# The first unit of the first product as eight plain products instead of seven combined ones

## The chip, the cores and the metric

The kernel runs on one core of a Trainium2 chip. The metric is the device time of one execution in microseconds (us); lower is better. "TensorE" or PE is the matrix engine, "VectorE" or DVE and "ScalarE" or ACT are the two engines that do sums, copies and the activation, POOL and SP mainly issue transfers (DMA).

## The reference

```python
# x: 16 x 512 x 768, w1: 768 x 3072, b1: 3072, w2: 3072 x 768, float32
y = np.matmul(x, w1) + b1
y = 0.5 * y * (1.0 + erf(y / np.sqrt(2.0)))        # GELU
return np.matmul(y, w2)
```

## The kernel before

The 8192 rows of x are worked on in blocks of 1024. In a block, the first product is cut into 12 units, one for each 256 columns of w1. A unit is a 2 x 2 block product: A11, A12, A21, A22 are quarters of the x block (512 rows by 384), B11 to B22 are quarters of the unit's weight (384 by 128). It is done with seven block products in place of eight, at the price of sums (a form of Strassen's scheme). On TensorE one block product is three matmuls of 128x512.

```python
# sums of x (DVE), made once for a block:     S1, S2, A21 (overwritten), S4
ops = ((S1, A21, A22, ADD), (S2, S1, A11, SUB), (A21, A11, A21, SUB), (S4, A12, S2, SUB))

# sums of the weight (DVE), made for each unit; T1 overwrites B12 in place
for d, a, b in ((T3, B22, T1), (T1, T1, B11), (T2, B22, T1), (T4, B21, T2)): ...   # d = a - b

# the seven products of a unit: p -> (operand from x, operand from the weight)
{1: (A11, B11), 2: (A12, B21), 3: (S4, B22), 4: (A22, T4),
 5: (S1, T1),   6: (S2, T2),   7: (A21, T3)}
```

The products go to six PSUM banks (bX and bY twice, bW, bZ); engine copies between banks (`copy_xy`: bX to bY; after P6: bY to bZ) let later products add to an earlier sum. Each unit overlaps with the one before it:

```python
def period(i, j, fill):              # i: this unit, j: the one before
    if i and i.g:
        p1(i); copy_xy(i)            # unit 0's P1 and P2 are done by the start code
    if j: p7(j)
    fill(1)                          # fill: DVE sums for later units, loads
    if i: p5(i)
    fill(2)
    if j: p3(j)
    fill(3)
    if i: p6(i)
    if j: j.right_done()             # GELU
    fill(4)
    if j: p4(j)
    fill(5)
    if i and i.g: p2(i)
    fill(6)
```

The start loads eight tiles of x (128 rows each) and the first weights, transposes the tiles on TensorE and copies them out of PSUM. Meanwhile "spins", matmuls on zeros that compute nothing, are there to keep TensorE busy, so that it keeps its clock.

```python
spin(9)
for t in range(4):
    ...                                       # cast tile t
    transpose_pe(0, t)
    spin(2 if t < 3 else 6)
nc.vector.tensor_copy(...)                    # weight 0, first half of its rows: cast by DVE
nc.scalar.copy(...)                           # second half: cast by ACT
prep_wt(0); flush(soon)                       # four subtractions on weight 0
first = Unit1(0, 0, 0)
p1(first, 0, KQ)
copy_xy(first)
for t in range(4, 8):
    transpose_pe(0, t, nc.vector.tensor_copy if t == 5 else nc.scalar.copy)
    if t % 2:
        x_sums(0, soon, top if t == 5 else bottom, (0, 1)); flush(soon)
    if t < 7:
        spin(2)
p2(first)
spin(3)
...                                           # other x sums; then period(first, None, ...)
```

## Time and profile before

| | before |
|---|---|
| median of the first three runs | 857.49 us (856.77 to 858.31) |
| span of the profiled run | 856.2 us |
| TensorE busy | 850.1 us, 99% |
| VectorE / ScalarE busy | 76% / 49% |

The profile's page first. Its busy row gives busy us, share of the span and number of instructions for each engine; the other row gives shares of the chain of waits, the chain of work that ended last.

```profile
PE 850.1 (99%) x6307; PEld 560.7 (65%) x6307; DVE 653.8 (76%) x1108; ACT 421.2 (49%) x682; POOL 80.6 (9%) x131
PE 97%; DMA 2%; ACT 0%; DVE 0%; SPq 0%; issue 0%
```

TensorE bounds the kernel. The table by stages says where it is not full: the columns are the stretch, its length, PE's busy time and matmuls, granted TensorE clock (1.00 is full), DMA share, GB/s.

```profile
0.00:20.00 20.00, 18.06 (x103) 1.00 1.08 227
20.00:40.00 20.00, 19.96 (x97) 1.00 1.29 193
```

Only the first 20 us have room, and a good part of what is busy there is spins. So the start is read one row at a time: start us, busy us, engine, source line, operation, output and input, count, and in brackets the engine's idle time before and what ended it. L663 is a spin, L294 a transpose, L369 a product of a unit.

```profile
13.96 0.51 PE L294 MATMUL bT<-ident,arena 128*128 128x128 f16 x6
14.31 0.81 PE L369 MATMUL bX<-arena 128*128 128x512 f16 x3
14.95 0.38 PE L663 MATMUL bY<-arena 128*128 128x512 f16 x1
15.17 0.38 PE L663 MATMUL bZ<-arena 128*128 128x512 f16 x1
15.38 0.38 PE L663 MATMUL bY<-arena 128*128 128x512 f16 x1
15.95 0.81 PE L369 MATMUL bW<-arena 128*128 128x512 f16 x3 [0.19 <-DVE arena L179]
16.59 0.81 PE L369 MATMUL bY<-arena 128*128 128x512 f16 x3
17.24 0.81 PE L369 MATMUL bX<-arena 128*128 128x512 f16 x3
18.06 0.81 PE L369 MATMUL bY<-arena 128*128 128x512 f16 x3
18.71 0.81 PE L369 MATMUL bW<-arena 128*128 128x512 f16 x3
...
23.44 0.81 PE L369 MATMUL bW<-arena 128*128 128x512 f16 x3
...
28.05 0.81 PE L369 MATMUL bW<-arena 128*128 128x512 f16 x3
```

The last tile is transposed at 13.96, P2 of unit 0 follows at 14.31, then three spins and a wait: P5 of unit 0 (bW, 15.95) needs the sum S1, which needs the copy of tile 7. Five products of unit 0 (P5, P6, P7, P3, P4) are still to do there. Because matmuls overlap, three of them advance the start of the next group by 0.65 us, not by the 0.81 shown. Each bW row is P5 of a unit: unit 0 at 15.95, unit 1 at 18.71, unit 2 at 23.44, unit 3 at 28.05. From there the distance is 4.53 us per unit: TensorE is full. So **P5 of unit 3** marks how much the start cost.

ScalarE's copy of tile 7 (L296) ends at 14.51 + 0.80 = 15.31:

```profile
10.30 0.83 ACT L676 CAST arena<-arena 128x768 f16<-128x768 f32 x1
...
14.51 0.80 ACT L296 COPY arena<-bT 128x768 f16<-128x768 f16 x1 [0.18 <-PE bT L294]
```

### The profile page before, as it was taken

Reading aid. Unit: us, or ns where it says so; the run is one execution under the profiler, and the core shown is the slowest. Engines: PE = TensorE matmul, PEld = TensorE weight load, DVE = VectorE, ACT = ScalarE, POOL = GpSimd, SP = SyncE. Lnnn points to the kernel's source line nnn. Section 1 sums busy time; section 2 is a strip of 40 time slices with the busy share of each in tenths; the row PEclk is TensorE's granted clock in tenths of the full one; section 3 lists DMA queues with packets and bytes.
Section 4 is the critical chain, followed back from the end, with each engine's and each line's share of the span. In section 5 each row is a group of like instructions: output and inputs, shape, how many; then the busy total and the mean of one; then the engine's idle time right before and its main releaser. Section 6 shows DMA issues by size and latency. Waiting matters only on the chain.

```text
span 856.2 us, 16201 instructions
## 1 busy us (share of the span) xinstructions
PE 850.1 (99%) x6307; PEld 560.7 (65%) x6307; DVE 653.8 (76%) x1108; ACT 421.2 (49%) x682; POOL 80.6 (9%) x131
## 2 busy tenths in 40 slices
PE   9999999999999999999999999999999999999998
PEld 4444445666544798448974499645995459944698
DVE  5765676756447998579986799677996689956998
ACT  5777762111177512875138732477215771267611
POOL 5021100000100001100020000200002100010000
PEclk9999999999999999999999999999999999999999
DMA  9996895659889798996979879897998959967398
GB/s 225 223 236 96 242 192 188 235 167 284 186 242 319 192 324 324 266 291 209 335 279 307 246 257 333 277 286 222 301 345 257 337 153 324 356 218 272 97 304 288
DMA packets 143265, 219.03 MB, mean 256 GB/s; under 512 B 61692, under 2 KB 84148, under 8 KB 143188
## 3 DMA queue, kind: packets, MB, share of 16 engines
q1 hardware_dynamic: 117968, 180.62, 65.6%
q0 software_dynamic: 25184, 37.36, 20.9%
q8 instruction: 49, 0.80, 0.4%
q14 instruction: 28, 0.23, 0.1%
q10 hardware_dynamic: 36, 0.01, 0.0%
HBM read 180.30 MB, written 47.87 MB: 266 GB/s over the span
## 4 chain that ended last, share of the span: by engine, by line
PE 97%; DMA 2%; ACT 0%; DVE 0%; SPq 0%; issue 0%
PE bY L369 21%; PE bY L461 15%; PE bX L369 14%; PE bX L461 10%; PE bW L369 7%; PE bZ L369 7%; PE bY L409 5%; PE bZ L461 5%; PE bW L461 5%; PE bX L409 4%; PE bZ L409 2%; PE bW L409 2%; DMA arena<-w1s 1%; DMA arena<-in_x_dram 1%; PE bT L294 0%; ACT arena L296 0%
## 5 line engine op out<-in xcount | busy, mean ns | idle before, releaser
L179 DVE TENSOR_TENSOR arena<-arena 128x768 f16<-128x768 f16 (+4 forms) x620 | 392.7, 664 | 10.6 <-PE bW L409 2.8
L369 PEld LDWEIGHTS <-arena 128*128 128x128 f16 x2016 | 196.5, 98 | 230.5 <-issue 1.3
L461 PEld LDWEIGHTS <-arena 128*128 128x128 f16 x3528 | 292.1, 98 | 8.3
L369 PE MATMUL bY<-arena 128*128 128x512 f16 x864 | 218.9, 379 | 0.1
L539 DVE TENSOR_TENSOR arena<-bY,arena 128x512 f32<-128x512 f32 (+1 forms) x104 | 70.8, 681 | 144.7 <-PE bY L369 88.7
L369 PE MATMUL bX<-arena 128*128 128x512 f16 x576 | 141.5, 379 | 0.6 <-DMA arena<-w1s 0.6
L532 ACT COPY bY<-bX 128x512 f32<-128x512 f32 (+1 forms) x146 | 80.3, 550 | 125.0 <-DVE arena L510 87.7
L385 ACT ACTIVATE arena<-arena,b1t 128x1024 f16<-128x1024 f32 x96 | 110.4, 1151 | 57.2 <-DVE arena L567 57.2
L461 PE MATMUL bY<-arena 128*128 128x192 f16 x1500 | 138.3, 246 | 0.0
L552 ACT COPY arena<-bW 128x512 f32<-128x512 f32 (+1 forms) x146 | 80.8, 553 | 95.1 <-PE bW L461 43.3
L409 PEld LDWEIGHTS <-arena 128*128 128x128 f16 x672 | 65.8, 98 | 44.2
L461 PE MATMUL bX<-arena 128*128 128x192 f16 x1020 | 93.1, 246 | 0.0
L567 DVE TENSOR_TENSOR arena<-bZ,arena 128x512 f32<-128x512 f32 (+1 forms) x104 | 70.7, 680 | 25.5 <-PE bZ L369 18.4
L369 PE MATMUL bW<-arena 128*128 128x512 f16 x288 | 77.8, 379 | 0.2 <-DVE arena L179 0.2
L369 PE MATMUL bZ<-arena 128*128 128x512 f16 x288 | 77.8, 379 | 0.0
L390 ACT ACTIVATE arena<-bX,b1t 128x512 f16<-128x512 f32 x96 | 65.4, 681 | 7.5 <-PE bX L369 7.5
L493 POOL DMA_DIRECT2D out_dram<-arena x42 | 30.6, 729 | 394.8 <-DVE arena L563 288.3
L390 ACT ACTIVATE arena<-bY,b1t 128x512 f16<-128x512 f32 x96 | 64.7, 674 | 0.0
L284 POOL DMA_DIRECT2D arena<-in_x_dram x60 | 32.4, 544 | 273.2 <-DMA arena<-arena 194.0
L585 DVE COPY bZ<-bY 128x512 f32<-128x512 f32 (+1 forms) x67 | 45.8, 683 | 6.1
L409 PE MATMUL bY<-arena 128*128 128x384 f16 x288 | 49.6, 326 | 0.0
L461 PE MATMUL bZ<-arena 128*128 128x192 f16 x504 | 48.5, 246 | 0.0
(43 smaller groups left out, 331.2 us busy)
## 6 DMA issues: line engine op xcount, KB each, us to landing
arena<-w2s SPq DMA_DIRECT2D x294, 288.0 KB, 4.6
arena<-w1s SPq DMA_DIRECT2D x72, 672.0 KB, 5.8
out_dram<-arena POOLq DMA_DIRECT2D x42, 384.0 KB, 4.8
w2s<-arena SPq DMA_DIRECT2D x49, 288.0 KB, 4.4
arena<-in_x_dram POOLq DMA_DIRECT2D x60, 192.0 KB, 6.7
w1s<-arena SPq DMA_DIRECT2D x12, 672.0 KB, 8.2
out_dram<-arena SPq DMA_DIRECT2D x21, 384.0 KB, 3.2
arena<-in_w_dram POOLq DMA_DIRECT2D x17, 384.0 KB, 8.1
```

The costliest lines, as they stand in the source:

```text
L179: nc.vector.tensor_tensor(out=o, in0=a, in1=b, op=op)
L284: nc.gpsimd.dma_start(out=xhs[t], in_=xr[:, sb * 8 + t, :])
L369: nc.tensor.matmul(out=dst[:, 0:RH], lhsT=w1_op(self.wt, slot)[:, c, :], rhs=a[:, c, :], start=first and c == 0, stop=c == self.C - 1, ski ...
L385: nc.scalar.activation(out=self.G[1][:, hi, :, :], in_=self.tmp, func=GELU, bias=b1t[:, 2 * hi + 1:2 * hi + 2])
L390: nc.scalar.activation(out=self.G[0][:, hi, row, :], in_=bank[:, 0:RH], func=GELU, bias=b1t[:, 2 * hi:2 * hi + 1])
L409: nc.tensor.matmul(out=dst[:, 0:N2], lhsT=a, rhs=w[:, :, c, :], start=first and c == 0, stop=c == self.C - 1, skip_group_check=True)
L461: nc.tensor.matmul(out=dst[:, t * N4:(t + 1) * N4], lhsT=a, rhs=w[:, c, :], start=first and c == 0 and t == ts[0], stop=c == NQ - 1, skip_ ...
L532: nc.scalar.copy(out=bY[u.g % 2][:, 0:u.F], in_=bX[u.g % 2][:, 0:u.F])
L539: nc.vector.tensor_tensor(out=u.c22(), in0=bY[u.g % 2][:, 0:u.F], in1=w[:, 0:u.F], op=ADD)
L552: nc.scalar.copy(out=w[:, 0:u.F], in_=bW[:, 0:u.F])
L567: nc.vector.tensor_tensor(out=u.c12(), in0=bZ[:, 0:u.F], in1=w[:, 0:u.F], op=ADD)
L585: nc.vector.tensor_copy(out=bZ[:, 0:u.F], in_=bY[u.g % 2][:, 0:u.F])
```

## The change

The intent: unit 0 of the first block is computed plainly, C = A1 B1 + A2 B2 with eight block products. That is one product more, but none waits for a sum, so some can be done while tiles 4 to 7 still arrive. Weight 0's subtractions leave the start; they are done at unit 3, because unit 0 of the second block needs them.

```diff
-            spin(2 if t < 3 else 6)
+            spin(2)
 ...
-        prep_wt(0)
-        flush(soon)
-        first = Unit1(0, 0, 0)
-        p1(first, 0, KQ)
-        copy_xy(first)
-        warm = warm[1:]
-        for t in range(4, 8): ...            # transposes, sums, spin(2)
-        p2(first)
-        spin(3)
+        def plain(dst, row, side, half):
+            slot = ((B11, T1), (B21, B22))[half][side]      # the T1 slot still holds B12
+            for c in range(KQ):
+                nc.tensor.matmul(out=dst[:, 0:RH], lhsT=w1_op(wts[0], slot)[:, c, :],
+                                 rhs=blocks(0)[2 * row + half][:, c, :],
+                                 start=half == 0 and c == 0, stop=half == 1 and c == KQ - 1, ...)
+        plain(bX[0], 0, 0, 0)
+        transpose_pe(0, 4)
+        plain(bX[0], 0, 0, 1)
+        transpose_pe(0, 5, nc.vector.tensor_copy)
+        x_sums(0, soon, top, (0, 1)); flush(soon)
+        transpose_pe(0, 6)
+        plain(bY[0], 0, 1, 0)
+        transpose_pe(0, 7)
+        x_sums(0, soon, bottom, (0, 1)); flush(soon)
+        plain(bY[0], 0, 1, 1)
+        spin(2)
+        for row, banks in enumerate(((bX[0], bY[0]), (bW, bZ))):
+            for side in range(2):
+                if row:
+                    plain(banks[side], row, side, 0)
+                    plain(banks[side], row, side, 1)
+                plain_done(banks[side], row, side)          # GELU straight from PSUM
+        prep_wt(1)
+        ...                                   # other x sums
 ...
             if slot == 4:
+                if pos == 3:
+                    prep_wt(0)
 ...                                          # cuts: unit 0 leaves the loop over units
```

The spins now write bX[1] and bY[1]. That is not cosmetic: P6 and P7 add to a value that ScalarE has copied into bY. The Trainium skill ("PSUM — Partial Sum Buffer", "The four PSUM rules") says that VectorE and ScalarE writes neither set nor clear the bits which decide whether a matmul adds or overwrites; a matmul adds to such a value where the bit is set, as it is after any matmul wrote there. A spin does that for bY[1], and the plain products do it for bY[0] and bZ.

More of the change, by code (lines that the diff above doesn't have):

```diff
@@ L577, in p6 @@
             u.mm(6, bY[u.g % 2], False, 0, u.C)
-            on_act = u.g == 0 or isinstance(u, Unit3) or (isinstance(u, Unit1) and u.sb >= ONE and u.g % 2)
+            on_act = isinstance(u, Unit3) or (isinstance(u, Unit1) and u.sb >= ONE and u.g % 2)
             if isinstance(u, Unit3) and u.add is not None:
@@ L610, in period @@
                 return
-            if i and i.g:
+            if i:
                 p1(i, 0, i.C)
@@ L630, in period @@
             fill(5)
-            if i and i.g:
+            if i:
                 p2(i)
@@ L657 @@
             load_wt(n)
-        warm = [bY[0], bY[1], bZ]
         def spin(n):
             for k in range(n):
-                nc.tensor.matmul(out=warm[k % len(warm)][:], lhsT=zero[:, 0, 0:P], rhs=zero[:, 0, :],
+                nc.tensor.matmul(out=(bX[1], bY[1])[k % 2][:], lhsT=zero[:, 0, 0:P], rhs=zero[:, 0, :],
                                  start=True, stop=True, skip_group_check=True)
@@ L673 @@
                 nc.scalar.copy(out=b1t[:], in_=bW[:, 0:2 * NH])
-            spin(2 if t < 3 else 6)
+            spin(2)
         nc.vector.tensor_copy(out=w1_raw(wts[0])[:, 0:KQ, :], in_=wf[:, 0:KQ, :])
         nc.scalar.copy(out=w1_raw(wts[0])[:, KQ:2 * KQ, :], in_=wf[:, KQ:2 * KQ, :])
-        prep_wt(0)
-        flush(soon)
-        first = Unit1(0, 0, 0)
-        p1(first, 0, KQ)
-        copy_xy(first)
-        warm = warm[1:]
-        top, bottom = slice(0, 2 * P), slice(2 * P, RH)
-        for t in range(4, 8):
-            transpose_pe(0, t, nc.vector.tensor_copy if t == 5 else nc.scalar.copy)
-            if t % 2:
-                x_sums(0, soon, top if t == 5 else bottom, (0, 1))
-                flush(soon)
-            if t < 7:
-                spin(2)
@@ L691 @@
-        p2(first)
-        spin(3)
-        for r in (top, bottom):
-            x_sums(0, soon, r, (2,))
-        flush(soon)
-        for r in (top, bottom):
-            x_sums(0, soon, r, (3,))
+        def plain(dst, row, side, half):
[3 more added lines that the diff above has]
+                                 rhs=blocks(0)[2 * row + half][:, c, :],
+                                 start=half == 0 and c == 0, stop=half == 1 and c == KQ - 1,
+                                 skip_group_check=True)
@@ new lines, in plain_done @@
+        def plain_done(dst, row, side):
+            nc.scalar.activation(out=Gs[0][side][:, 0, row, :], in_=dst[:, 0:RH], func=GELU,
+                                 bias=b1t[:, side:side + 1])
+        top, bottom = slice(0, 2 * P), slice(2 * P, RH)
+        plain(bX[0], 0, 0, 0)
+        transpose_pe(0, 4)
+        plain(bX[0], 0, 0, 1)
+        transpose_pe(0, 5, nc.vector.tensor_copy)
+        x_sums(0, soon, top, (0, 1))
+        flush(soon)
+        transpose_pe(0, 6)
+        plain(bY[0], 0, 1, 0)
@@ new lines @@
+        transpose_pe(0, 7)
+        x_sums(0, soon, bottom, (0, 1))
+        flush(soon)
+        plain(bY[0], 0, 1, 1)
[7 more added lines that the diff above has]
+        prep_wt(1)
+        last = [soon.pop()]
+        for k in (2, 3):
+            for r in (top, bottom):
+                x_sums(0, soon, r, (k,))
@@ L700 @@
+        flush(soon)
+        soon += last
         seq = ([(0, k) for k in range(7)] +
@@ L732, in fill_a @@
             if slot == (1 if pos < at[1, 0] else 4) and pos + 1 < len(seq) and seq[pos + 1][0] == 0:
-                s4 = [soon.pop(0), soon.pop(0)] if pos == 0 else []
                 prep_wt(seq[pos + 1][1])
-                soon[2:2] = s4
             if slot == 4:
+                if pos == 3:
+                    prep_wt(0)
                 for m, c in ((21, 9), (22, 0), (23, 3), (23, 6)):
@@ L755, in fill_a @@
                     sums((0, 1100, 0, 0, 1500)[slot])
-            elif slot in (1, 2, 4, 5) and (pos, slot) != (0, 2):
+            elif slot in (1, 2, 4, 5):
                 sums((0, 600, 300, 0, 600, 300)[slot])
@@ L905 @@
         for g, (kind, sb, k) in enumerate(units):
-            cur = kind(g, sb, k) if g else first
+            if g == 0:
+                loads_a(0)
+                continue
+            cur = kind(g, sb, k)
             if g < len(seq):
```

## The prediction

> **What bounds the kernel.** TensorE: 850.1 of 856.2 us busy (99%, busy table), 97% of the chain of waits, granted clock 1.00. By the stage table PE is full from 20 us to the tail, except 0.6 us at a weight reload. Only the first 20 us (PE 18.06 busy, partly warm-up "spins" that compute nothing) can give time back; afterwards PE runs at a fixed period (timeline: 4.53 us per seven-product unit).
>
> **Removed, added, moved** (timeline of the first 30 us; a product, three 128x512 matmuls, takes 0.65 us; six transposes 0.33; a spin 0.21).
> Unit 0 goes from 7 to 8 products (+0.65 us of PE), but they need no sums. Before, PE filled the waits for x tiles 4 to 7 (transposes at 11.35, 12.11, 12.98, 13.96; the last two waited for loads), for the copy of tile 7 (ends 15.31) and for the first sum with 9 spins; when that sum was done (15.95), five products of unit 0 were left. After, three more products fit between the transposes, so at the copy of tile 7 (about 15.3, fixed by the same loads) four are left, ending near 18.0.
>
> Then unit 1: P1 at 18.0, P5, P6 (waits about 0.2 us for the ScalarE copy, queued behind four GELUs), P2, then P1 of unit 2, P7 of unit 1, and P5 of unit 2 at about 22.2. Before it started at 23.44, and P5 of unit 3 at 28.05; I expect the latter at 26.7 to 27.1, 1.0 to 1.35 us earlier.
>
> DVE loses four subtractions of weight 0 there (1.54 us); they come back at units 3 to 4. DVE then has 3.6 + 1.5 us of work in a 4.53 us period, lagging about 0.5 us, against slack of about 0.45 us at the copy to bZ and 1 us at the c22 sum: cost to PE 0 to 0.2 us. DVE is the risk earlier too: six x sums (0.52 each), weight-1 subtractions (0.36 each) and the first bZ copy (0.7), which P7 of unit 1 waits for, end near 21.4, just when PE gets there (21.45). Weights 1, 2, 3 seem to land at 16.2, 18.2, 20.2 (POOL's waits), early enough.
>
> **Critical path.** All the PE gain is on it; nothing later absorbs it, as later loads are issued from program positions. The Trainium skill ("TensorE: Matmul & The Clock Gate", Part 1) says that PE needs about 3.4 us of sustained activity for full rate and loses it after an idle window as long. The trace agrees with the first: spins are 0.43 us apart until about 5 us, then 0.21. Idle gaps after stay under 0.7 us, so I expect no loss.
>
> **Predicted:** 856.3 us (gain 1.2, 0.14%), range 855.2 to 857.4, which includes the run-to-run spread (856.8 to 858.3 before). Faster by over 2%: 0.003; within 2%: 0.992; slower by over 2%: 0.005.
>
> **Shown right by:** first product near 10.5; row-1 products from about 15.4 to 18.0 without gap; P5 of unit 3 around 27; two PE matmuls fewer in all (3 more, 5 spins fewer); period still 4.53 at units 4 and 5. **Shown wrong by:** a PE wait above 0.4 us on DVE at unit 1's bZ copy, a stall at the deferred weight-0 subtractions, waits on weight loads, or matmuls at 0.43 us (clock lost).
>
> **What would make it wrong.** DVE or ScalarE queue order costing more than 0.2 us at units 1 to 4, eating the gain to about 0; or the clock falling with fewer spins (+1 to 3 us).

## The result, and the profile after

Four sets of executions were made, each with before and after on the same chip. All are fast: none is over 1.5% above the fastest of its kernel. All outputs are right. The ratio is the mean time of one kernel's fast runs over that of the other's fast runs of the same rounds, so not quite the ratio of the medians.

| set | before: median (runs) | after: median (runs) | ratio, 95% interval |
|---|---|---|---|
| 1, the result | 857.58 (4) | 856.54 (4) | 0.9989, 0.9970 to 1.0008 |
| 2, run after_again | 858.72 (11) | 856.22 (6) | 0.9985, 0.9969 to 1.0002 |
| 3, run after_third | 858.49 (11) | 857.67 (6) | 0.9998, 0.9979 to 1.0018 |
| 4, run after_fourth | 857.73 (9) | 856.07 (5) | 0.9978, 0.9965 to 0.9992 |

The mean of all 21 runs after is 856.98, of all 35 before 858.11: 1.1 us less (0.13%), with a standard error of 0.4 us worked out from the spread of both groups; without the one run of 862.01 us it is 1.4 us.

The same two rows of the page, and of the table by stages, after:

```profile
PE 848.3 (99%) x6299; PEld 560.3 (66%) x6299; DVE 652.0 (76%) x1106; ACT 419.6 (49%) x680; POOL 81.1 (9%) x131
PE 98%; DMA 1%; POOL 0%; issue 0%; DVE 0%
```

```profile
0.00:20.00 20.00, 17.89 (x101) 1.00 1.08 227
20.00:40.00 20.00, 20.00 (x103) 1.00 1.28 197
```

Note the trap: TensorE is *less* busy in the first 20 us than before. Busy time does not show the gain, as a spin counts as busy. The rows of the timeline do (L680 is a plain product, L662 a spin):

```profile
14.07 0.51 PE L294 MATMUL bT<-ident,arena 128*128 128x128 f16 x6
14.42 0.81 PE L680 MATMUL bY<-arena 128*128 128x512 f16 x3
15.07 0.38 PE L662 MATMUL bX<-arena 128*128 128x512 f16 x1
15.28 0.38 PE L662 MATMUL bY<-arena 128*128 128x512 f16 x1
15.50 1.46 PE L680 MATMUL bW<-arena 128*128 128x512 f16 x6
16.80 1.46 PE L680 MATMUL bZ<-arena 128*128 128x512 f16 x6
18.09 0.81 PE L369 MATMUL bX<-arena 128*128 128x512 f16 x3
18.74 0.81 PE L369 MATMUL bW<-arena 128*128 128x512 f16 x3
19.56 0.81 PE L369 MATMUL bY<-arena 128*128 128x512 f16 x3
...
21.50 0.81 PE L369 MATMUL bY<-arena 128*128 128x512 f16 x3
22.15 0.81 PE L369 MATMUL bW<-arena 128*128 128x512 f16 x3
...
26.68 0.81 PE L369 MATMUL bW<-arena 128*128 128x512 f16 x3
```

Four products of unit 0 are left at 15.50 and end at 18.09 without a gap. P5 of units 1, 2, 3 starts at 18.74, 22.15, 26.68. ScalarE's copy of tile 7 ends at 14.62 + 0.80 = 15.42:

```profile
14.62 0.80 ACT L296 COPY arena<-bT 128x768 f16<-128x768 f16 x1 [0.20 <-PE bT L294]
```

So the *stretch* from the end of that copy to P5 of unit 3 fell from 28.05 - 15.31 = 12.74 us to 26.68 - 15.42 = 11.26 us, by 1.48. Three parts make it up:

- Before, TensorE took up unit 0's remainder 0.64 us after the copy (15.95), waiting for a sum; after, 0.08 us (15.50). 0.56 us.
- From there to P5 of unit 3 there are 18 products before and 17 after. One product is 0.65 us (4.53 / 7).
- 18 products are 11.65 us of the 12.10 between 15.95 and 28.05, so 0.45 us were gaps; 17 are 11.0 of the 11.18 after, so 0.18 (P6 of unit 1 waits 0.17, at 19.56). 0.27 us.

The first and the third part are read from these rows; no run changed one of them alone.

VectorE after, first behind the copy of tile 7 and then at unit 3, where the deferred subtractions are:

```profile
15.45 5.09 DVE L179 TENSOR_TENSOR arena<-arena 128x768 f16<-128x768 f16 x12 [0.65 <-ACT arena L296]
...
20.47 0.70 DVE L585 COPY bZ<-bY 128x512 f32<-128x512 f32 x1
...
30.00 1.79 DVE L179 TENSOR_TENSOR arena<-arena 128x384 f16<-128x384 f16 x5
31.71 0.68 DVE L539 TENSOR_TENSOR arena<-bY,arena 128x512 f32<-128x512 f32 x1
```

VectorE has no gap from 15.45 until 21.8. The copy to bZ, for which P7 of unit 1 waits, ends at 21.17, and P7 starts at 21.50: 0.33 us of slack. At 30.00 five subtractions stand where there was one, and no idle time is left before the c22 sum (31.71), which adds the banks that P7 and P5 of a unit left; before, it was 1.13 us:

```profile
32.85 0.69 DVE L539 TENSOR_TENSOR arena<-bY,arena 128x512 f32<-128x512 f32 x1 [1.13 <-PE bY L369]
```

The two first profiles differ by 2.1 us, more than the start explains (1.37 by the clock). The rest is a wait of the profile before, for a weight that is fetched again (w1s), that the first profile after happens not to have. The product before it starts at 384.07, so this one is 1.39 - 0.65 = 0.74 us late; the idle time in brackets, 0.57, is less, as it counts from the modelled end of a matmul:

```profile
385.46 0.82 PE L369 MATMUL bX<-arena 128*128 128x512 f16 x3 [0.57 <-DMA arena<-w1s]
```

### The profile page after: what moved, and what is told of

It reads as the page before. It is cut to its first block, busy times and chain, and to the rows that moved or that the text cites. A ratio compares the mean times of both kernels' runs of the same rounds, so it can differ in the third digit from the quotient of the medians.

```text
span 854.1 us, 16173 instructions
## 1 busy us (share of the span) xinstructions
PE 848.3 (99%) x6299; PEld 560.3 (66%) x6299; DVE 652.0 (76%) x1106; ACT 419.6 (49%) x680; POOL 81.1 (9%) x131
## 4 chain that ended last, share of the span: by engine, by line
PE 98%; DMA 1%; POOL 0%; issue 0%; DVE 0%
PE bY L369 22%; PE bY L461 15%; PE bX L369 14%; PE bX L461 10%; PE bZ L369 7%; PE bW L369 7%; PE bY L409 5%; PE bZ L461 5%; PE bW L461 5%; PE bX L409 4%; PE bZ L409 2%; PE bW L409 2%; DMA arena<-in_x_dram 1%; POOL arena L284 0%; PE bT L294 0%; PE bY L680 0%
## 5 line engine op out<-in xcount | busy, mean ns | idle before, releaser
L369 PE MATMUL bY<-arena 128*128 128x512 f16 x855 | 216.7, 379 | 0.0
L369 PE MATMUL bX<-arena 128*128 128x512 f16 x570 | 139.7, 379 | 0.0
```

The lines of the kernel that those rows point to most:

```text
L369: nc.tensor.matmul(out=dst[:, 0:RH], lhsT=w1_op(self.wt, slot)[:, c, :], rhs=a[:, c, :], start=first and c == 0, stop=c == self.C - 1, ski ...
```

## The experiments

The whole time scatters by more than the effect, so the verdicts rest on one profile each and on the stretch defined above, which leaves out when tile 7 came. The table has every profile. "Rest" is span minus P5 of unit 3; "reload" is the recorded idle time of TensorE on w1s, which is smaller than the delay it stands for (0.57 for 0.74 above).

| run | copy of tile 7 ends | stretch | rest | reload | span |
|---|---|---|---|---|---|
| before | 15.31 | 12.74 | 828.15 | 0.57 | 856.2 |
| before_again | 16.97 | 12.74 | 827.49 | 0 | 857.2 |
| before_third | 15.19 | 12.74 | 828.27 | 0.57 | 856.2 |
| after | 15.42 | 11.26 | 827.42 | 0 | 854.1 |
| after_again | 15.20 | 11.26 | 827.94 | 0.50 | 854.4 |
| after_third | 15.97 | 11.26 | 828.87 | 1.19 | 856.1 |
| after_fourth | 15.26 | 11.26 | 827.58 | 0 | 854.1 |
| fewer_spins | 15.45 | 12.73 | 829.22 | 1.12 | 857.4 |
| two_moved | 16.94 | 12.56 | 827.70 | 0.29 | 857.2 |
| sums0_early | 15.05 | 12.40 | 829.05 | 1.32 | 856.5 |
| row1_halves | 15.53 | 10.88 | 831.69 | 2.85 | 858.1 |
| halves_act | 15.16 | 10.21 | 828.93 | 0.39 | 854.3 |
| halves_act_2 | 14.95 | 10.21 | 829.54 | 0.84 | 854.7 |
| halves_wq | 15.56 | 10.21 | 828.73 | 1.23 | 854.5 |

The theory: the copy of tile 7 fixes when the rest can run, and the change leaves fewer products, and no sum, behind it. Rivals: the gain comes from spins taken out of TensorE's way; from the plain form wherever it stands; from the deferral of weight 0's subtractions alone; or the difference of the totals is only scatter.

### The two kernels again

> The kernel before once more, for the spread of the start in the profile. P5 of unit 3 (the bW product near 28 us) started at 28.05 us in the first profile; every theory expects 28.05 within 0.15. The wait of 0.74 us on a weight reload near 385 us need not come back, as it is taken to be chance; if it comes back at the same place, it belongs to the kernel.

> The changed kernel once more, with more executions. P5 of unit 3 started at 26.68 us in its first profile: 26.7 within 0.15 expected. If the gain is the 1.37 us of the start and nothing else, the ratio of times is 0.9984 (856.2 for 857.6). If the whole 2.1 us of the two first profiles belonged to the change, 0.9975.

Both stretches came back to 0.01 us. But before_again was 1.66 us late at P5 of unit 3 (29.71, where I expected 28.05 within 0.15: a miss), with the whole delay ahead of the copy of tile 7. ScalarE in before_again:

```profile
12.73 0.83 ACT L676 CAST arena<-arena 128x768 f16<-128x768 f32 x1 [2.37 <-DMA arena<-in_w_dram]
13.46 0.58 ACT L532 COPY bY<-bX 128x512 f32<-128x512 f32 x1
13.98 0.79 ACT L296 COPY arena<-bT 128x768 f16<-128x768 f16 x1
```

The second half of weight 0 came at 12.7 us, where the first profile had it by 10.3. The copy of tile 4 (13.98), whose transposes had begun at 11.49, had to wait behind that cast. The Trainium skill ("TensorE: Matmul & The Clock Gate", Part 1, on queue depths) says that the queues of ACT and DVE are strictly first in, first out; these rows agree. The reload wait near 385 us was absent here, so it is not a fixed part of the kernel before. The ratio of after_again, 0.9985, is the one that the start alone gives (0.9984).

### Fewer spins

```diff
 # in the kernel before
-            spin(2 if t < 3 else 6)
+            spin(2)
-            if t < 7:
-                spin(2)
-        spin(3)
+        spin(2)
```

> The kernel before with 19 spins in place of 30 (as many as after), still seven combined products. Theory (the copy of x tile 7 and then the first sum set the start, spins only fill waits): P5 of unit 0 stays at 15.95 and P5 of unit 3 at 28.05, within 0.15. Rival (the gain comes from the spins taken out of TensorE's way): P5 of unit 3 comes up to 1.3 us earlier, near 26.7. If the clock falls for lack of work, matmuls at 0.43 us show it.

The stretch was 12.73 us, as in the kernel before; P5 of unit 0 started at 16.09, the copy of tile 7 ended 0.14 us later than in the first profile, and P5 of unit 3 at 28.18. No product ran at the slow rate. The spins only fill waits; taking eleven out gains nothing.

### Two products moved back behind tile 7

```diff
 # in the kernel after
-        plain(bY[0], 0, 1, 0)
+        spin(3)
         transpose_pe(0, 7)
 ...
-        plain(bY[0], 0, 1, 1)
+        spin(3)
         spin(2)
 ...
-                if row:
+                if row or side:
```

> The kernel after with the two products of the second side of row 0 (bY) moved from between the transposes to behind the copy of tile 7; three spins stand in each one's old place. The same eight products, so the same work. Theory (what counts is how many products are left when tile 7 is there): six in place of four are left, P5 of unit 3 comes 2 x 0.648 = 1.30 us later, at 27.98 (0.1 to 0.2 less if the moved products close an existing wait). Rival (the plain form itself, without sums and copies, brings the gain, wherever it stands): stays at 26.7 within 0.3.

By the clock P5 of unit 3 started at 29.50, but this execution again had the late weight half (the copy of tile 7 ended at 16.94). Counted from there the stretch was 12.56 us, 1.30 more than the 11.26 of the kernel after: two products at 0.65, to the hundredth. That the late weight itself does not change the stretch is known from before_again. So eight plain products bring nearly nothing (0.18 us) if two more of them stand behind tile 7; what counts is how many are left there. This run also has the deferred subtractions, so the deferral alone is not the gain either. The copy of tile 7 and P5 of unit 3:

```profile
16.14 0.80 ACT L296 COPY arena<-bT 128x768 f16<-128x768 f16 x1 [0.18 <-DVE arena L179]
...
29.50 0.81 PE L369 MATMUL bW<-arena 128*128 128x512 f16 x3
```

### Weight 0's subtractions back at the start

```diff
 # in the kernel after: behind the x sums of the start, no longer at pos 3
+        prep_wt(0)
         flush(soon)
         soon += last
```

> The kernel after with the four subtractions of weight 0 put back into the start (before the last subtraction of weight 1) in place of unit 3. If the deferral matters: VectorE runs without a gap from 15.45 to 20.5 us in the kernel after, and 4 x 0.36 = 1.44 us more push the copy to bZ of unit 1 from 20.47 to 21.9 and P7 of unit 1 from 21.50 to 22.65, a TensorE wait of about 1.1 us; P5 of unit 3 at 27.8 or a little later. Rival (VectorE has room there, deferral only tidies): P5 of unit 3 stays at 26.7 within 0.2.

VectorE's row of sums was four longer, and TensorE waited. The rows are VectorE's, then TensorE's:

```profile
15.09 6.53 DVE L179 TENSOR_TENSOR arena<-arena 128x768 f16<-128x768 f16 x16 [0.68 <-ACT arena L296]
21.53 0.69 DVE L585 COPY bZ<-bY 128x512 f32<-128x512 f32 x1
```

```profile
22.28 0.81 PE L369 MATMUL bY<-arena 128*128 128x512 f16 x3 [0.98 <-DVE bZ L585]
```

P7 of unit 1 waited 0.98 us, and the stretch rose by 1.14 to 12.40 us, which leaves 0.34 of the gain of 1.48. P5 of unit 3 by the clock was 27.45, below the 27.8 that I gave, as tile 7 was copied 0.37 us earlier here. Against this place the deferral is a needed part of the change, though it shows no gain of its own: VectorE had 0.33 us of room there, and 1.4 us of work would have gone into it. Note that the run does not put them where they stood before (11.17 us, ahead of tile 5): T1 overwrites B12, which the plain products still read until 17.4 us. VectorE stood idle for 3.02 us there in the kernel after (until 12.99), so with a buffer of its own for T1 they might fit; no run tried that.

### Going further: the second row in halves

```diff
 # in the kernel after; plain_cols does 256 of the 512 columns, tiles 4 and 5 (top) or 6 and 7
         plain(bX[0], 0, 0, 0)
+        plain(bY[0], 0, 1, 0)
         transpose_pe(0, 4)
 ...
         transpose_pe(0, 7)
 ...
-        spin(2)
+        plain_cols(bW, 0, top)
+        plain_cols(bZ, 1, top)
 ...                                # behind the copy of tile 7 only plain_cols(..., bottom)
```

> A try to go further: the kernel after with its second-row products cut into two halves of 256 columns, the half for tiles 4 and 5 done before the copy of tile 7 in place of the last two spins, and one product of row 0 moved ahead of tile 4. TensorE alone would finish unit 0 at 17.0 in place of 18.09. If VectorE's unbroken row of sums (to 20.5 us) and the copy to bZ behind it are the next limit, P7 of unit 1 still waits until about 21.1 to 21.2, and P5 of unit 3 gains only 0.3 to 0.5 (26.2 to 26.4). If TensorE's own row is the limit, it gains 1.0 (25.7).

> As row1_halves, and the copy to bZ of unit 1 is done by ScalarE, so it need not queue behind VectorE's sums. If VectorE's queue was the limit of row1_halves, P5 of unit 3 comes at 25.6 to 25.8, 0.9 to 1.1 us ahead of the kernel after; time against the kernel before 0.9972 (2.4 us). If not, it equals row1_halves.

> halves_act again, beside halves_wq and the kernel after on one chip. The stretch from the copy of tile 7 to P5 of unit 3 was 10.21 us, 1.05 below the kernel after: 10.2 within 0.05 again, and a median 1.0 us below the kernel after (or up to 0.5 away from that by the spread of the weight reloads).

`halves_act` adds one line: `on_act` is also true for unit 1, so ScalarE makes its copy to bZ. Two halves share one bank here; only the first matmul in the bank carries the start flag, because a second one would clear the first half's bits as well (the same page and section on PSUM). The results were correct; no run tried it with a second flag.

row1_halves finished unit 0 at 17.15, as planned, and then waited on VectorE, whose copy to bZ ended at 21.17:

```profile
21.23 0.81 PE L369 MATMUL bY<-arena 128*128 128x512 f16 x3 [0.51 <-DVE bZ L585]
```

Its stretch, 10.88 us, is 0.38 below the kernel after, the 0.3 to 0.5 of the VectorE theory. With the copy on ScalarE the wait was gone and the stretch 10.21 us, 1.05 below the kernel after, in three profiles. P5 of unit 3 came at 25.37 us in halves_act, earlier than the 25.6 to 25.8 that I gave, as tile 7 was copied 0.26 us earlier too. But in two of the three profiles nearly all of it was handed back. In halves_act, VectorE at unit 5, then TensorE a little later:

```profile
36.56 1.14 DVE L179 TENSOR_TENSOR arena<-arena 128x384 f16<-128x384 f16 x3 [1.16 <-DMA arena<-in_w_dram]
```

```profile
41.88 1.46 PE L369 MATMUL bY<-arena 128*128 128x512 f16 x6 [0.62 <-ACT bY L532]
```

VectorE now stood still until weight 5 arrived at 36.5 us, and it fell behind with its other work; the c22 sum of the next unit came late, and with it TensorE: the product that waits at 41.88 starts at 42.24 in the first profile after, so of the lead of 1.31 us at P5 of unit 3 only 0.36 is left. halves_act_2 shows the same (waits of 1.32 and 0.62 us, a lead of 1.52 us cut to 0.41); halves_wq, whose start came 0.4 to 0.6 us later by the clock, does not. In these profiles the load sets a second time that did not move with the start (36.50, 36.56, and 36.94 in row1_halves). In the whole times, the ratios to the kernel before were 0.9978 (0.9965 to 0.9992) and 0.9969 (0.9956 to 0.9982), medians 856.59 and 855.41 us. That beats the kernel before; against the kernel after it is ahead in the one set that they share (set 3: 855.41 against 857.67), but the intervals of the ratios overlap and the advantage is not settled. The 2.26 us there are also more than the 0.5 to 1.5 us that I expected of halves_act_2, a miss whose cause is open; after_third has the run of 862.01 us. The single time of row1_halves, 859.87 us, came with 2.85 us of reload waits. Set beside the first profile after, matmul by matmul from P5 of unit 3, it falls back by 0.29 us at unit 5, where VectorE waited 0.51 us for weight 5, and by 4.0 us at five places between 379 and 590 us where TensorE turns to a reloaded weight; in three of them the wait is recorded.

### The late half of weight 0

```diff
 # in halves_act
-            nc.sync.dma_start(out=wf[:, r, :], ...)
+            (nc.sync, nc.scalar)[half].dma_start(out=wf[:, r, :], ...)
```

> halves_act with the second half of weight 0 fetched through ScalarE's queue at the very start, in place of last on SyncE's. In two profiles of nine this half was there only at 12.7 us and ScalarE's cast of it held back the copies behind it, so that everything came 1.5 to 1.7 us later. Theory (that late landing makes the upper of the two groups of times): the half is there by 10 us, the times fall in one group with less spread, and the median is 0.3 to 1.0 us below halves_act. Rival (the late landing is only a matter of bytes, so another transfer will be late in its place): an x tile lands later, and times and spread are as in halves_act.

In its profile the half was there when ScalarE came to it (10.4 us), but the second x tile came later (its cast at 6.54 us against 5.12 in the first profile after). Five of its six times lay between 854.84 and 856.29 us, one at 859.01; the median, 855.97, lay 0.6 *above* halves_act_2 in the same set. The gain that I expected was not there. The late landing was seen in two profiles of fourteen; whether it makes all the slower times, most of which have no profile, stays open.

### Is the gain kept?

> The changed kernel a third time, for the whole time. Theory (1.48 us gained at the start, from the copy of tile 7 to P5 of unit 3: 12.74 us before, 11.26 after, and kept to the end): ratio 0.9983, and that stretch 11.26 within 0.05 again. Rival (the gain is given back in some executions): ratio above 0.9995.

> The kernel before once more, for its waits on weight reloads beside those of the kernel after: 0.6 and 0 us in its two profiles so far. The stretch from the copy of tile 7 to P5 of unit 3 is 12.74 within 0.05. If reload waits are chance, anything from 0 to 1.3 us; if they come of the earlier start, under 0.7.

> The changed kernel a fourth time, because its ratio in the third set (0.9998) lay above the 0.9983 that the start alone gives. If the 1.48 us of the start are kept and the rest is the spread of early loads and weight reloads, the stretch is 11.26 again and the ratio over all sets together stays between 0.9975 and 0.9995. Rival (the earlier start gives time back at the weight reloads): the reload waits of TensorE in this profile are above 1 us, as in the third (1.2), and the ratio is again near 1.

The third set gave a ratio of 0.9998, a miss, and by its number the outcome that I had given to the rival: the six times ran from 855.77 to 862.01 us. Its profile had the same stretch, 11.26 us; tile 7 was copied 0.55 us later than in the first profile after, and the reload waits were 1.19 us. The fourth set gave 0.9978 and no reload wait. Take the recorded reload waits out of the rest, and it is 827.5 to 827.7 us in the three profiles before and 827.4 to 827.7 in the four after: the 1.48 us are kept in these profiles. (fewer_spins, the same kernel as before from there on, has 828.1, so this measure is good to some 0.5 us.) Reload waits were 0.57, 0 and 0.57 us before, and 0, 0.50, 1.19 and 0 after; with so few I cannot exclude that an earlier start changes their odds a little. What made the run of 862.01 us is open: it was not profiled.

## Why the prediction was right

- *What bounds the kernel, and where the room is.* Right: only the first 20 us changed, and the difference reached the end.
- *"Five products left" against "four".* Right, and the core of it: two_moved put two back and lost 2 x 0.65 us exactly. The first sum's wait, 0.56 us, was the other large part, read from the rows.
- *The times.* Row 1 from 15.50 to 18.09 (predicted 15.4 to 18.0), P6 waiting 0.17 (0.2), P5 of unit 2 at 22.15 (22.2), P5 of unit 3 at 26.68 (26.7 to 27.1). I took 1.0 to 1.35 us of gain; it was 1.37 by the clock, just outside, and 1.48 counted from tile 7, as I had kept 0 to 0.2 us for VectorE's lag that was not needed.
- *The deferred subtractions.* Right: VectorE's idle time before the c22 sum went from 1.13 us to none, and TensorE's period stayed 4.53 us (26.68, 31.21, 35.74).
- *VectorE as the first risk.* Right, with 0.33 us of slack where I saw 0.05; sums0_early used it up and stalled TensorE for 0.98 us.
- *"Two PE matmuls fewer in all".* Wrong: eight fewer (6307 to 6299). I took five spins fewer, and it is eleven (30 to 19). It did not matter for the time: fewer_spins took the same eleven out and its stretch was unchanged.
- *"Nothing later absorbs it."* Right for this gain, but with less reserve than I thought: VectorE found weight 5 there only at 36.5 to 36.9 us in four profiles, and in after_fourth, one of them, it already waited 0.32 us for it (until 36.87), without a recorded wait of TensorE, though set beside the first profile after it falls 0.19 us back by 47 us. The next microsecond (halves_act) did meet it.
- *The clock.* Matmuls went from 0.43 to 0.21 us apart in each profile and no product ran slow after the first tiles, as predicted. But the prediction had the change too early: in the profile before, the six transposes at 5.17 us still took 0.82 us (0.50 for the six at 6.68), and the spins at 6.15 stood 0.31 us apart, so it came some 5 us after the first matmul at 1.19, not 3.4. The loss of the clock in a long gap was not met: two_moved idled 1.84 us before a product at 13.63, which took 0.82 us as at full rate, and no run tried a gap of 3.4 us.
- *The total.* 856.54 us against 856.3 predicted. One median of four runs could not have told a gain of 1.2 us from none; the stretch could.

## What to carry to other kernels

At the start of a kernel, ask how much real work is left when the last load is there, and move work that depends on the earlier loads ahead of it; a form with more arithmetic but fewer dependences can win there, though it costs a product more (0.65 us) where TensorE is full. Taking sums out of the start only helps if the engine that makes them also gets rid of them there: check that the engine next in line has slack, because 1.4 us of VectorE work put back cost 1.14 us. When the effect is smaller than the scatter of the whole time, find an event inside the profile that a load has just released, and measure from there: this repeated within 0.01 us where the whole times of one set lay 0.5 to 6.2 us apart.

## What the Trainium skill lacked or had wrong

- "TensorE: Matmul & The Clock Gate", Part 1, puts the change to full rate about 4 us into sustained activity, give or take 0.5; further down it gives 6, 11 or 14 slow matmuls for one kernel in different runs, which is wider. Here the first matmul was at 1.19 us in every profile, and spins went from 0.43 to 0.21 us apart at about 4.1 us in halves_act_2 and only after 6.4 us in after: 2.9 to more than 5.2 us of activity, with the same spins up to 4.6 us. The give or take of 0.5 is too narrow here; the wider spread is the one to plan for.
- "DMA: Bandwidth & Descriptors" has no figure that I found for how much the landing of one and the same transfer at a kernel's start moves between executions. Here weight 0's second half was there by 11.0 us in eleven profiles and at 12.7 us in two, of the thirteen that fetch it through the same queue, which moved everything behind it by 1.5 to 1.7 us.
